# Two heads' scores interleaved from both halves of TensorE's rows, buffers rearranged, and a pinned order in the grouped-query stage

## The chip, the cores and the metric

One NeuronCore of one Trainium2 chip runs the whole program. The metric is device microseconds of one execution. The kernel before took 1280.51 us as the median of three runs, from 1273.82 to 1281.13.

The engines are named as in the profile: PE is TensorE's matmuls, PEld its weight loads, DVE is VectorE, ACT is ScalarE, POOL is GpSimd and SP is SyncE, which issues the DMAs. A line number such as L175 is a line of the kernel before.

## What is computed

The reference is a two-layer encoder on x of 512 tokens by 1024 channels (float32), with four kinds of attention, each with 8 query heads of 64 channels:

- Layer 0, A: attention over the 128 best keys of each query, chosen by an indexer whose scores are sums over 4 small heads; B: chunked attention with a learned bias by distance. Both outputs are concatenated, projected and added to x.
- Layer 1, C: causal attention whose logits get F[t] - F[s], a cumulated log forget gate; D: a sliding window with sinks, where 8 query heads share 2 key heads (grouped queries, 4 heads to a key head). Concatenated, projected, added.
- After each mixer a gated MLP with a causal depthwise convolution, and RMSNorm ahead of every block and at the end.

In every head the logits are q.k over 64 channels, then a softmax over the keys, then P.v. Blocks of 128 queries are used; block i needs keys 0 to 128(i+1), so its logits are 128 x 128(i+1).

## The kernel before

**Precision and matmuls.** Every float32 operand is split into a high and a low part of a reduced format. A product takes three matmuls (`mm3`, L174 to L177): high x high, high x low, low x high, all into one accumulator bank of 128 x 512 (PSUM has 8 banks; `banks` gives 3 to the tag "acc", 3 to "s" and 2 to "tp").

**Weights.** `Stream` loads weights in the order of `PLAN`, 128 x 1024 at a time, through SP's queue into two "raw" buffers; ACT makes the high part (L135) and DVE, for two kinds POOL, the low part (L137). `W.ahead(2)` keeps up to two loads ahead of use.

**Fill work.** Projections are written as Python generators. `Fill.step(n)` runs n steps; one step is three 512-column matmuls for the projections (q and k of the next heads, the queries of D, v of A, output projections). Fill is set between the parts of the attention heads, so that TensorE has work while ACT, DVE and POOL do a softmax. The numbers of steps are written by hand: `FILL_B`, `FILL_A`, `FILL_C`, `FILL_D`.

**A head (B, A and C).** `Head.score` makes four score tiles, of 128, 256, 384 and 512 columns, in three "s" banks, 12 matmuls in all. A pair of heads shares a tile `qk`: head 0 lies in partitions 0 to 63, head 1 in 64 to 127 (`r0`), so that a score matmul uses 64 of the 128 rows of the array. `Head.soft` adds the bias and takes the minimum (DVE), exponentiates (ACT), takes the reciprocal (DVE) and scales (POOL). `Head.turn` transposes P on TensorE into a "tp" bank and `hilo` (L181 to L183) splits it: ACT writes the high part, DVE the low part. `Head.av` multiplies by v into an "acc" bank and `Head.store` sums the two halves of that bank with ACT and DVE.

`weave(prev, cur, fill, n)` (L462) sets the order for one head: transposes of the head before, scores and softmax of this head, then fill in three parts with the remaining transposes and the P.v of the head before in between.

The top-128 choice of A (`topk`, L608 and L609, on DVE) is written behind the B heads. In the trace it runs from 46 to 146 us, beside B.

**C's bias.** `bias_c` selects one row of F with a matmul of 40 rows (`sel`, L874) into a "tp" bank; ACT and POOL make the four bias tiles of one head from it.

**D.** `Unit(i, g)` treats one block of 128 queries and one key head: 12 score matmuls of 64 rows, in two "s" banks, softmax of four heads, transposes, P.v into an "acc" bank. The key head g picks the row half (`r`). Eight units follow one another, with fill of the output projection of C between them.

**What sets the order.** A framework schedules the program: it simulates it, and on each engine issues what is ready, by the order of the source where several are. So an engine's instruction order is that of the simulated schedule and not of the source, while each engine runs its own queue strictly in order. The matmuls of the indexer (L579 to L584), which do the same for its own heads as the change does for the attention heads, show this: they are written in pairs, one matmul for each row half, into two banks:

```
for pas, (x, y) in enumerate(((0, 0), (0, 1), (1, 0))):
    for e in range(2):
        r = slice(64 * e, 64 * e + 64)
        nc.tensor.matmul(ss_[e], iq[r, x, hp, i * 128:w], ik[r, y, 0, 0:w], ...
```

and in the trace some of them stand in this order and some with all three of one e first.

Of the kernel before, what the change touches and what calls it, by code (L numbers as in the profile page):

```python
# [61 lines left out]
def ffn_plan(layer):  # L62
# [4 lines left out]
    for g in range(NFF):  # L67
# [18 lines left out]
def trunk(ctx, tc, a, out):  # L86
# [9 lines left out]
    banks = {"acc": 3, "s": 3, "tp": 2}  # L96
# [4 lines left out]
    h = hp.tile([128, KD, SEQ], F32, name="h")  # L101

    def load_x(c):
        nc.sync.dma_start(h[:, c, :], a["x"][:, c, :])
# [69 lines left out]
    def mm3(o, lh, ll, rh, rl, start, stop):  # L174
        nc.tensor.matmul(o, lh, rh, start=start, stop=False)  # L175
        nc.tensor.matmul(o, lh, rl, start=False, stop=False)  # L176
        nc.tensor.matmul(o, ll, rh, start=False, stop=stop)  # L177
# [20 lines left out]
    for i in range(9):  # L198
        nc.tensor.matmul(wt[:, :128], ones, ones, start=i == 0, stop=i == 8)
# [3 lines left out]
    def squares(c):  # L203
        if c == 0:
            hold_ss["t"] = sp.tile([128, SEQ], F32, name="scr2", tag="scr2", bufs=2)
            nc.scalar.activation(hold_ss["t"], h[:, 0, :], AF.Square, scale=1.0 / 32.0)
            return
        ss = hold_ss["t"]
        sq = sp.tile([128, SEQ], F32, name="os", tag="os", bufs=1)
        nc.scalar.activation(sq, h[:, c, :], AF.Square, scale=1.0 / 32.0)  # L210
# [3 lines left out]
    def squares_ahead():  # L214
        a2 = None
        for p in range(KD // 2):
            sq = sp.tile([128, 2, SEQ], F32, name="scr", tag="scr")
            nc.scalar.activation(sq, h[:, 2 * p:2 * p + 2, :], AF.Square, scale=1.0 / 32.0)
# [8 lines left out]
    def absorb(c, n, sq=True):  # L227
        g = gT[:, n, c:c + 1]
        nc.scalar.activation(xT[0][:, c, :], h[:, c, :], AF.Copy, scale=g)  # L229
        nc.vector.scalar_tensor_tensor(xT[1][:, c, :], h[:, c, :], g, xT[0][:, c, :].bitcast(F32),  # L230
                                       op0=OP.mult, op1=OP.subtract)
        if sq:
            squares(c)

    def token_roots():
        pt = bank("tp", (128, NT))
        for t in range(NT):
            nc.tensor.matmul(pt[:, t:t + 1], hold_ss["t"][:, t * 128:(t + 1) * 128], ones[:, 0:1],  # L238
# [3 lines left out]
    def roots(t0=0, t1=NT, copy=True):  # L242
# [5 lines left out]
        nc.tensor.matmul(pr[:, :n], ones, dg[:, :n], start=True, stop=True)  # L248
# [95 lines left out]
    def add_resid(c, o, cols=slice(0, SEQ)):  # L344
        nc.vector.tensor_tensor(h[:, c, cols], o[:, cols], h[:, c, cols], OP.add)  # L345
# [46 lines left out]
    class Head:  # L392
        def __init__(self, mp, job, ybufs):
            self.mp, self.job, self.ybufs = mp, job, ybufs
            self.where = {}

        def begin(self):
            self.nm = smp.tile([128, NT], F32, name="nm", tag="s4")
            self.sm = smp.tile([128, NT], F32, name="sm", tag="s4")
            P = self.mp.tile([128, 1280], F32, name="P", tag="P", bufs=2)  # L400
            self.L = [P[:, 64 * i * (i + 1):64 * (i + 1) * (i + 2)] for i in range(NT)]

        def score(self):
            qk, r0 = self.job["qk"], self.job["r0"]
            both = bank("s")
            self.s = [both[:, 0:128], both[:, 128:384], bank("s")[:, :384], bank("s")]
            for i, s in enumerate(self.s):
                w = 128 * (i + 1)
                q0, q1 = [qk[r0:r0 + 64, b, 0, i * 128:w] for b in range(2)]
                k0, k1 = [qk[r0:r0 + 64, b, 1, 0:w] for b in range(2)]  # L410
                mm3(s, q0, q1, k0, k1, True, True)

        def soft(self, i):
            s = self.s[i]
            L, nm, sm = self.L[i], self.nm[:, i:i + 1], self.sm[:, i:i + 1]
            nc.vector.tensor_tensor_reduce(out=L, in0=s, in1=self.job["bias"][i], scale=1.0, scalar=3e38,
                                           op0=OP.add, op1=OP.min, accum_out=nm)
            nc.scalar.activation(L, L, AF.Exp, scale=-1.0, bias=nm, accum_out=sm)
            nc.vector.reciprocal(sm, sm)
            nc.gpsimd.tensor_scalar(L, L, sm, 1.0, op0=OP.mult, op1=OP.mult)  # L420

        def turn(self, pk):
# [3 lines left out]
            for j in pk:  # L426
                at[j] = off
                for i in range(j, NT):
                    nc.tensor.transpose(pt[:, off:off + 128], self.L[i][:, j * 128:(j + 1) * 128], ident)
                    off += 128  # L430
            th = self.mp.tile([128, 512], F32R, name="PTh", tag="PTh", bufs=3)
            tl = self.mp.tile([128, 512], F32R, name="PTl", tag="PTl", bufs=3)
            hilo(th[:, :off], tl[:, :off], pt[:, :off])
            for j in pk:
                self.where[j] = (th, tl, at[j])

        def av(self, js, first, last):
            if first:
                self.o = bank("acc")
            for j in js:  # L440
                th, tl, off = self.where[j]
                n = 512 - 128 * j
                v = self.job["V"][:, j].rearrange("p a d -> p (a d)")
                st, sp_ = first and j == js[0], last and j == js[-1]
                nc.tensor.matmul(self.o[:, j * 128:512], v, th[:, off:off + n], start=st, stop=False)
                nc.tensor.matmul(self.o[:, j * 128:512], v, tl[:, off:off + n], start=False, stop=sp_)

        def store(self):
            job, o = self.job, self.o
            e = job["e"]  # L450
# [696 lines left out]
```

## Time and profile before

| | |
|---|---|
| runs | 1273.82, 1280.51, 1281.13 us |
| profiled execution | 1283.04 us, of which the profile's span is 1281.3 us |
| busy in the span | PE 98%, PEld 80%, DVE 64%, ACT 46%, POOL 15% |
| matmuls | 5904 |
| mean granted TensorE clock | 0.986 of full speed |

The span has these stretches: to 72 us loading, the indexer and v of B; 72 to 150 us the B heads; 150 to 290 us the A heads; then layer 0's MLP; 690 to 718 us layer 1's first projections; 718 to 820 us the C heads; 820 to 884 us D; then output projection and MLP. A busy time is the union of the instructions' times; a matmul's time includes its way through the array, so that the distance between the starts of neighbours, not their duration, is what one costs in a row of many.

### The profile page before, as it was taken

The page shows a single profiled execution, that of the slowest core. Times are in us where ns is not written, and L with a number is a line of the kernel's source. Part 1 is how long each engine was busy: PE and PEld are TensorE (multiplying, and loading weights), DVE is VectorE, ACT ScalarE, POOL GpSimd, SP SyncE. Part 2 cuts the span into 40 slices and gives each one's busy share as a digit, 9 for nine tenths or more (in the row PEclk, how much of TensorE's full clock was granted, in tenths as well). Part 3 has the DMA queues.
Part 4 walks back from the last instruction along what each step waited for, and adds up shares of the span by engine and source line. Part 5 has one row for each costly group of instructions (what it writes and reads, how often), then busy time and mean ns, then how long its engine had stood idle before and what let it go on. Part 6 is the DMA issues. An engine that isn't in the chain of part 4 may idle for free. (4 is left out here: it accounts for less than half of the span.)

```text
span 1281.3 us, 15910 instructions
## 1 busy us (share of the span) xinstructions
PE 1256.6 (98%) x5904; PEld 1028.6 (80%) x5904; DVE 824.4 (64%) x1524; ACT 589.1 (46%) x1008; POOL 196.2 (15%) x275
## 2 busy tenths in 40 slices
PE   8999999999999999999999999999999999999997
PEld 7778878787888888888888777778788888888886
DVE  7989866667777777743325556677777777772222
ACT  6445455455544444432224556566544444442221
POOL 3446412212000000000011334212200000000000
PEclk9989999998999999999999999899999999999999
DMA  6222022312233333332222311211223333332221
GB/s 209 83 83 89 28 66 66 99 50 85 85 97 98 99 99 99 99 97 93 92 69 78 116 50 34 66 34 48 89 98 99 99 99 99 98 97 90 96 80 66
DMA packets 34221, 109.61 MB, mean 86 GB/s; under 512 B 4064, under 2 KB 6496, under 8 KB 34144
## 3 DMA queue, kind: packets, MB, share of 16 engines
q1 hardware_dynamic: 34144, 108.60, 26.6%
q8 instruction: 46, 0.75, 0.2%
q14 instruction: 31, 0.25, 0.1%
HBM read 106.49 MB, written 2.10 MB: 85 GB/s over the span
## 5 line engine op out<-in xcount | busy, mean ns | idle before, releaser
L137 DVE TENSOR_TENSOR wlo<-raw,whi 128x1024 fp32r<-128x1024 f32 (+2 forms) x188 | 233.3, 1242 | 152.6 <-ACT whi L135 149.6
L135 ACT ACTIVATE whi<-raw 128x1024 fp32r<-128x1024 f32 (+2 forms) x196 | 204.6, 1044 | 216.3 <-PE acc L176 139.3
L175 PE MATMUL acc<-xT,whi 128*128 128x512 f32 x480 | 189.9, 396 | 0.4 <-ACT xT L229 0.4
L176 PE MATMUL acc<-xT,whi 128*128 128x512 f32 x480 | 188.4, 392 | 1.8 <-DVE xT L230 1.8
L177 PE MATMUL acc<-xT,wlo 128*128 128x512 f32 x480 | 187.9, 391 | 0.0
L212 POOL TENSOR_TENSOR scr<-scr,os 128x512 f32<-128x512 f32 x24 | 34.3, 1430 | 724.5 <-ACT os L210 724.5
L177 PE MATMUL acc<-act,wlo 128*128 128x512 f32 (+1 forms) x374 | 140.9, 377 | 0.0
L175 PE MATMUL acc<-act,whi 128*128 128x512 f32 (+1 forms) x374 | 140.9, 377 | 0.0
L176 PE MATMUL acc<-act,whi 128*128 128x512 f32 (+1 forms) x374 | 140.9, 377 | 0.0
L175 PE MATMUL s<-xT,whi 128*128 128x512 f32 x352 | 139.0, 395 | 0.0
L176 PE MATMUL s<-xT,whi 128*128 128x512 f32 x352 | 137.9, 392 | 0.0
L177 PE MATMUL s<-xT,wlo 128*128 128x512 f32 x352 | 137.8, 392 | 0.0
L175 PEld LDWEIGHTS acc<-xT,whi 128*128 128x128 f32 x480 | 90.8, 189 | 23.1 <-issue 4.1
L176 PEld LDWEIGHTS acc<-xT,whi 128*128 128x128 f32 x480 | 90.9, 189 | 21.0 <-DVE xT L230 2.5
L177 PEld LDWEIGHTS acc<-xT,wlo 128*128 128x128 f32 x480 | 90.7, 189 | 19.2
L175 PE MATMUL acc<-whi,xT 128*128 128x512 f32 (+2 forms) x208 | 83.6, 404 | 1.1 <-ACT whi L135 0.8
L710 DVE TENSOR_TENSOR ov<-s,R 128x512 f32<-128x512 f32 x44 | 30.4, 692 | 80.0 <-PE s L177 80.0
L177 PE MATMUL acc<-whi,xT 128*128 128x512 f32 (+2 forms) x208 | 80.7, 389 | 1.0 <-DVE xT L230 1.0
L182 ACT ACTIVATE act<-scr 128x512 fp32r<-128x512 f32 x44 | 27.8, 631 | 115.7 <-DVE scr L734 115.7
L176 PE MATMUL acc<-wlo,xT 128*128 128x512 f32 (+2 forms) x208 | 80.5, 388 | 0.4 <-DVE wlo L137 0.4
L177 PEld LDWEIGHTS acc<-act,wlo 128*128 128x128 f32 x374 | 70.4, 188 | 13.0
L175 PEld LDWEIGHTS acc<-act,whi 128*128 128x128 f32 x374 | 70.4, 188 | 12.9
(230 smaller groups left out, 2351.2 us busy)
## 6 DMA issues: line engine op xcount, KB each, us to landing
raw<-in_w SPq DMA_DIRECT2D x188, 512.0 KB, 3.5
h<-in_x SPq DMA_DIRECT2D x8, 256.0 KB, 3.9
T<-in_relb SPq DMA_DIRECT2D x8, 256.0 KB, 2.7
raw<-in_w_i SPq DMA_DIRECT2D x4, 324.0 KB, 3.6
raw<-in_w_d SPq DMA_DIRECT2D x4, 264.0 KB, 2.7
out_y<-h SPq DMA_DIRECT2D x4, 256.0 KB, 2.2
out_y<-h SPq DMA_DIRECT2D x2, 384.0 KB, 2.4
ropeC<-in_ropeC SPq DMA_DIRECT2D x2, 256.0 KB, 4.6
```

The lines of the kernel that those rows point to most:

```text
L135: nc.scalar.activation(hi[:, :w], raw[:, :w], AF.Copy)
L137: eng.tensor_tensor(lo[:, :w], raw[:, :w], hi[:, :w].bitcast(F32), OP.subtract)
L175: nc.tensor.matmul(o, lh, rh, start=start, stop=False)
L176: nc.tensor.matmul(o, lh, rl, start=False, stop=False)
L177: nc.tensor.matmul(o, ll, rh, start=False, stop=stop)
L182: nc.scalar.activation(dh, src, AF.Copy)
L212: eng.tensor_tensor(ss, ss, sq, OP.add)
L710: nc.vector.tensor_tensor(v, o, R, OP.mult)
```

## The change

- **Heads in pairs.** `Head` becomes `Pair`. `Pair.score` issues the 24 score matmuls of two heads. Head 0 goes through its tiles in the order 256, 384, 128, 512 columns, head 1 in 384, 128, 512, 256; the two lists are merged by the columns that each has behind it. Each is put behind the matmul traced before it by `tc.keep_in_program_order` (an order of issue on the engine, no wait). The scores fill four "s" banks and two "tp" banks (the 256-column tiles); the two heads never share a bank.
- **Units in pairs.** `Unit(i)` takes both key heads; its 24 score matmuls alternate between the row halves, each pair of the same size, in four "s" banks.
- **Buffers.** "acc" has 2 banks and "s" 4. P.v goes to a "tp" bank. The softmax of a pair is in pieces (`begin`, `rest`, `soft(e, rows)`), the 256-column row first, so that P has a small buffer with four copies and a large one with two; the split transposes have 2 buffers of 512 columns and 1 of 256 where there were 3 of 512. VB (v of B) takes the place of the residual `h`, and x is loaded once more (8 DMAs on SP) after the first A pair.
- **`weave`** has seven parts of fill with shares `PARTS` (D: `PARTS_D`), and the step counts are new. `topk` no longer stands behind a full run of the fill; v of A, the second q and k group of A and B's output projection are in one fill list.
- **C's bias.** `forget_row` uses 128 rows and an "s" bank, and three matmuls a pair (512, 256 and 512 columns) where there were two of 512.
- **D pinned.** From the weave of C's last pair with D's first unit on, `pe.pinned` puts every TensorE instruction behind the one traced before it, until D's units are done.

The core of the diff:

```diff
-FILL_B = (9, 11, 9, 8, 8, 19, 8, 7)
-FILL_A = (22, 17, 10, 10, 11, 6, 5, 3)
-FILL_C = (6, 15, 11, 8, 8, 9, 7, 15)
-FILL_D = ((1, 1, 1, 1), (1, 1, 1, 1), (1, 1, 2, 0), (1, 1, 1, 1),
-          (1, 1, 1, 1), (1, 1, 1, 1), (0, 2, 2, 2), (1, 2, 2, 0))
+FILL_B = (8, 20, 21, 22, 22)
+FILL_A = (23, 30, 16, 14, 11)
+FILL_C = (6, 18, 16, 15, 12)
+FILL_D = (10, 9, 9, 9, 8)
+PARTS = (0, 20, 40, 50, 60, 72, 90, 100)
+PARTS_D = (0, 35, 45, 55, 55, 90, 100, 100)
...
-    banks = {"acc": 3, "s": 3, "tp": 2}
+    banks = {"acc": 2, "s": 4, "tp": 2}
...
+    class Ordered:
+        pinned = False
+        def _do(self, fn, *x, **kw):
+            ins = fn(*x, **kw)
+            if self.pinned:
+                tc.keep_in_program_order(ins)
+            return ins
...
+        def score(self):
+            qk = self.job["qk"]
+            one = [bank("tp") for _ in range(2)]
+            two = [bank("s") for _ in range(2)]
+            three = [bank("s") for _ in range(2)]
+            self.s = [[two[e][:, 0:128], one[e][:, :256], two[e][:, 128:512], three[e]]
+                      for e in range(2)]
+            todo = []
+            for e, order in ((0, (1, 2, 0, 3)), (1, (2, 0, 3, 1))):
+                at = 0
+                for i in order:
+                    for n, (b, c) in enumerate(((0, 0), (0, 1), (1, 0))):
+                        todo.append((at, e, i, n, b, c))
+                        at += i + 1
+            last = None
+            for _, e, i, n, b, c in sorted(todo):
+                w = 128 * (i + 1)
+                r = slice(64 * e, 64 * e + 64)
+                ins = pe.matmul(self.s[e][i], qk[r, b, 0, i * 128:w], qk[r, c, 1, 0:w],
+                                       start=n == 0, stop=n == 2)
+                if last is not None:
+                    tc.keep_in_program_order(ins)
+                last = ins
...
+        if prev is not None:
+            prev.turn(0, 0)
         if cur is not None:
             cur.score()
+            for e in range(2):
+                cur.begin(e)
+                cur.soft(e, (1,))
+        if prev is not None:
+            prev.turn(0, 1)
+        if cur is not None and cur.early:
+            for e in range(2):
+                cur.rest(e)
+                cur.soft(e, (2, 0, 3))
         fill.step(parts[0])
+        if prev is not None:
+            prev.turn(0, 2)
+        if cur is not None and not cur.early:
+            cur.rest(0)
+            cur.soft(0, (2, 0, 3))
+        if prev is not None:
+            prev.av(0, 0)
         fill.step(parts[1])
         if prev is not None:
+            prev.av(0, 1)
+            prev.store(0)
+        if mid is not None:
+            mid(0)
         fill.step(parts[2])
+        if prev is not None:
+            prev.turn(1, 0)
+        fill.step(parts[3])
+        if prev is not None:
+            prev.turn(1, 1)
+        fill.step(parts[4])
...
-        VB = mp.tile([128, NT, 8, 2, HD], F32R, name="VS", tag="VS", bufs=1)
+        VB = hp.tile([128, NT, 8, 2, HD], F32R, name="VB", tag="h")
...
+            if p == 0:
+                H["h"] = hp.tile([128, KD, SEQ], F32, name="h", tag="h")
+                for c in range(KD):
+                    load_x(c)
...
+        def forget_row(hh, w):
+            sel = mp.tile([128, 128], F32R, name="sel", tag="PSh", bufs=1)
...
+            pb = bank("s")
+            pe.matmul(pb[:, :w], sel, FTh[:, :w], start=True, stop=True)
...
+                for u in range(2):
+                    for e in range(2):
+                        for n, (b, c) in enumerate(((0, 0), (0, 1), (1, 0))):
+                            for g in range(2):
+                                r = slice(64 * g, 64 * g + 64)
+                                ins = pe.matmul(self.s[u][g][:, e, :nk], qd[u][r, b, e, qs],
+                                                       kdT[r, c, k0:k0 + nk], start=n == 0, stop=n == 2)
...
+        for i in range(NT + 1):
...
+            pe.pinned = True
+            cur = Unit(i) if i < NT else None
+            weave(pend, cur, fill, FILL_D[i], share=PARTS_D if i else PARTS)
+            pend = cur
+        pe.pinned = False
```

## Rows read from the trace of the kernel before

**Rows 1.** Windows, one stretch of the MLP: length, busy time (count) by engine, clock, DMA.
```profile
360.00:400.00 40.00, 40.00 (x178) 33.14 (x177) 29.06 (x37) 18.31 (x23) 0.00 (x0) 1.00 0.29 93
```

**Rows 2.** Windows, layer 0's heads, and within them the first 10 us and 92 to 142.
```profile
72.00:292.00 220.00, 214.67 (x1075) 174.54 (x1076) 167.73 (x444) 112.69 (x255) 72.24 (x100) 0.98 0.21 65
72.00:82.00 10.00, 7.07 (x19) 5.52 (x20) 8.47 (x29) 4.42 (x10) 3.30 (x6) 0.66 0.26 81
92.00:142.00 50.00, 50.00 (x261) 41.40 (x259) 48.81 (x139) 26.63 (x63) 32.82 (x40) 1.00 0.25 80
```

**Rows 3.** Windows, C and D, and within them 830 to 840.
```profile
718.00:884.00 166.00, 162.02 (x786) 123.40 (x785) 111.37 (x325) 106.94 (x275) 55.01 (x102) 0.96 0.15 48
830.00:840.00 10.00, 10.00 (x41) 7.90 (x40) 5.96 (x23) 4.77 (x16) 1.10 (x3) 0.68 0.12 48
```

**Rows 4.** Waits of PE: waiting <- releaser, us in total, times, longest.
```profile
PE s L175 <- ACT qk L491: 2.2, 2, 1.9
PE s L176 <- POOL qk L492: 2.1, 2, 1.1
...
PE acc L445 <- ACT PTh L182: 1.6, 1, 1.6
```

**Rows 5.** Timeline of PE, scores of one B head: start, length, what, count.
```profile
87.58 0.32 PE L175 MATMUL s<-qk 64*128 64x128 f32 x1
...
89.68 0.50 PE L175 MATMUL acc<-xT,whi 128*128 128x512 f32 x1
...
91.86 0.38 PE L429 MATMUL tp<-ident,P 128*128 128x128 f32 x2
```

**Rows 6.** Timeline of PE, the indexer's scores, window 55.50 to 55.60.
```profile
55.54 0.50 PE L582 MATMUL s<-qk 64*128 64x512 f32 x2
```

**Rows 7.** Timeline of PE, the same, window 56.28 to 56.30.
```profile
56.11 0.40 PE L582 MATMUL s<-qk 64*128 64x512 f32 x2
```

**Rows 8.** Timeline of PE, the same, window 56.51 to 56.54.
```profile
56.34 0.39 PE L582 MATMUL s<-qk 64*128 64x512 f32 x1
```

**Rows 9.** Timeline of PE, scores of one unit of D.
```profile
844.67 0.38 PE L175 MATMUL s<-kdT,qk 64*128 64x256 f32 x1
...
846.30 0.50 PE L175 MATMUL acc<-yT,whi 128*128 128x512 f32 x1
```

**Rows 10.** Timeline of PE, last score matmul of a parted C head, and next fill.
```profile
733.31 0.50 PE L177 MATMUL s<-qk 64*128 64x512 f32 x1
733.73 0.50 PE L175 MATMUL acc<-xT,whi 128*128 128x512 f32 x1
```

**Rows 11.** Timeline of PE, what parts the first parted head (in A).
```profile
176.03 0.63 PE L429 MATMUL tp<-ident,P 128*128 128x128 f32 x4 [0.29 <-DVE qk L183]
```

**Rows 12.** Timeline of PE, what parts the last parted head (in C).
```profile
806.66 0.66 PE L429 MATMUL tp<-ident,P 128*128 128x128 f32 x4
```

**Rows 13.** Timeline of PE, one selection of F for a C head.
```profile
758.98 0.50 PE L874 MATMUL tp<-FTh,sel 40*128 40x512 f32 x1
759.41 0.66 PE L429 MATMUL tp<-ident,P 128*128 128x128 f32 x4
```

**Rows 14.** Tile tp: duration in ns min/median/max, first and last start.
```profile
L182 ACT ACTIVATE PTh<-tp x86: 359/592/617, 87.2 to 882.3; 128x512 fp32r<-128x512 f32 x62, 128x256 fp32r<-128x256 f32 x24
L183 DVE TENSOR_TENSOR PTl<-tp,PTh x86: 395/680/692, 88.4 to 883.1; 128x512 fp32r<-128x512 f32 x62, 128x256 fp32r<-128x256 f32 x24
```

**Rows 15.** Groups of DVE, window 820 to 884: count, busy us, mean ns.
```profile
L956 DVE CUSTOM_DVE_ANT_0 P<-s,dmask,nsink 128x256 f32<-128x256 f32 x24 | 10.9, 477 | 1.6 <-PE s L177 1.6
...
L1003 DVE TENSOR_TENSOR Y<-acc,Y 64x512 f32<-64x512 f32 x7 | 4.8, 688 | 2.5 <-ACT Y L1002 2.4
```

**Rows 16.** Line 609, the choice of the top keys: durations, first and last start.
```profile
L609 DVE MATCH_REPLACE8 wk<-m,wk x48: 401/543/679, 46.5 to 145.7; 128x256 f32<-128x256 f32 x16, 128x384 f32<-128x384 f32 x16, 128x512 f32<-128x512 f32 x16
```

**Rows 17.** DMA issues: count, KB each, median us to landing.
```profile
raw<-in_w SPq DMA_DIRECT2D x188, 512.0 KB, 3.5
h<-in_x SPq DMA_DIRECT2D x8, 256.0 KB, 3.9
```

More of the change, by code (lines that the diff above doesn't have):

```diff
@@ L198, in trunk @@
     for i in range(9):
-        nc.tensor.matmul(wt[:, :128], ones, ones, start=i == 0, stop=i == 8)
+        pe.matmul(wt[:, :128], ones, ones, start=i == 0, stop=i == 8)
     hold_ss = {}
@@ L247, in roots @@
         pr = bank("tp", (128, NT, 128))
-        nc.tensor.matmul(pr[:, :n], ones, dg[:, :n], start=True, stop=True)
+        pe.matmul(pr[:, :n], ones, dg[:, :n], start=True, stop=True)
         if copy:
@@ L390, in load_rope @@
         nc.sync.dma_start(ropeS, a["ropeS"])
-    class Head:
+    class Pair:
         def __init__(self, mp, job, ybufs):
             self.mp, self.job, self.ybufs = mp, job, ybufs
[L395 to L401, printed above, removed]
-        def score(self):
[L404 to L407, printed above, removed]
-                w = 128 * (i + 1)
[L409 to L422, printed above, removed]
@@ L423, in turn @@
+        def turn(self, e, n):
+            pk = ([0], [1, 3], [2])[n]
             pt = bank("tp")
@@ L433, in turn @@
+            th = self.mp.tile([128, w], F32R, name=tag + "h", tag=tag + "h", bufs=bufs)
+            tl = self.mp.tile([128, w], F32R, name=tag + "l", tag=tag + "l", bufs=bufs)
             hilo(th[:, :off], tl[:, :off], pt[:, :off])
             for j in pk:
[L435 to L446, printed above, removed]
@@ L448, in store, with av @@
-        def store(self):
-            job, o = self.job, self.o
-            e = job["e"]
+                self.where[e][j] = (th, tl, at[j])
+        def av(self, e, n):
+            if n == 0:
+                self.o[e] = bank("tp")
+            o = self.o[e]
+            for j in ([0, 1, 3], [2])[n]:
+                th, tl, off = self.where[e][j]
+                w = 512 - 128 * j
+                v = self.job["V"](e)[:, j].rearrange("p a d -> p (a d)")
+                pe.matmul(o[:, j * 128:512], v, th[:, off:off + w], start=j == 0, stop=False)
+                pe.matmul(o[:, j * 128:512], v, tl[:, off:off + w], start=False, stop=j == 2)
@@ new lines, in trunk, with next_b, f @@
+        nb = {hh: bias_b(hh)() for hh in range(2)}
+        fill.step(FILL_B[0])
+        def next_b(p):
+            def f(e):
+                if p < 3:
+                    nb[2 * p + 2 + e] = bias_b(2 * p + 2 + e)()
+            return f
+        for p in range(4):
+            job = dict(qk=pairs[p]["qk"], pair=pairs[p], V=lambda e, p=p: VB[:, :, 2 * p + e],
+                       bias=[nb.pop(2 * p + e) for e in range(2)])
+            cur = Pair(mp, job, 2)
+            weave(pend, cur, fill, FILL_B[p + 1], next_b(p))
+            pend = cur
@@ new lines, in trunk @@
+        for i in (1, 2, 3):
+            topk(i)
+        later.drain()
+        for p in range(4):
+            if p == 2:
+                later.drain()
+            job = dict(qk=qkA[p], pair=pairs[4 + p], V=lambda e, p=p: VA["t"][:, :, 2 * p + e],
+                       bias=[[cmask, work[1], work[2], work[3]]] * 2)
+            cur = Pair(mp, job, 2)
+            weave(pend, cur, fill, FILL_A[p])
+            if p == 0:
+                H["h"] = hp.tile([128, KD, SEQ], F32, name="h", tag="h")
+                for c in range(KD):
+                    load_x(c)
+            pend = cur
@@ L697, in trunk @@
         fill.add(out_half("oA", lambda k: pairs[4 + k]["y"], after=lambda c: absorb(c, 1), lead=(0, 1, 2)))
-        weave(pend, None, fill, 11)
+        weave(pend, None, fill, FILL_A[4])
         fill.run()
@@ L912, in trunk, with next_c, f @@
         pend = None
-        nb = {0: bias_c(0)()}
-        fill.step(2)
-        for hh in range(8):
-            p = hh // 2
-            job = dict(qk=pairs[p]["qk"], r0=64 * (hh % 2), e=hh % 2, pair=pairs[p],
-                       V=VC[:, :, hh], bias=nb.pop(hh))
-            head = Head(mp, job, 1)
-            weave(pend, head, fill, FILL_C[hh])
-            if hh < 7:
-                nb[hh + 1] = bias_c(hh + 1)()
-            pend = head
-        fill.run()
+        bias_first(0)
+        fill.step(FILL_C[0])
+        def next_c(p):
+            def f(e):
+                if e == 0:
+                    bias_second(p)
+                elif p < 3:
+                    bias_first(p + 1)
+            return f
+        for p in range(4):
+            job = dict(qk=pairs[p]["qk"], pair=pairs[p], V=lambda e, p=p: VC[:, :, 2 * p + e], bias=cbias[p])
+            cur = Pair(mp, job, 1)
+            weave(pend, cur, fill, FILL_C[p + 1], next_c(p))
+            pend = cur
         Yds = {}
@@ L976, in turn @@
+            def turn(self, g, n):
                 if n >= len(self.blocks):
```

343 lines of the change are left out of this document (166 added, 177 removed).

## The prediction

> **What bounds the kernel now.** I read first the windows of the trace. In a stretch of the MLP TensorE starts 178 matmuls of 512 columns in 40 us at full clock: 0.225 us each, without a pause [rows 1]. The change doesn't touch those stretches. In layer 0's heads TensorE is busy 214.67 of 220 us and the clock is 0.98 of full [rows 2]; in C and D it is busy 162.02 of 166 us and the clock 0.96 [rows 3]. So TensorE bounds the attention stages too, and time can come from three places: fewer matmul slots, less lost where TensorE changes between kinds of matmul, and the idle and slow-clock time. The last is small: 5.3 + 4.0 us idle, and (220 x 0.02) + (166 x 0.04) = 11.0 us by the clock, 20.3 us together. The list of waits says what the idle time waited for: mostly the first heads' q and k, and one P.v on ACT [rows 4].
>
> **What a head's scores cost.** The 12 score matmuls of a B head begin at 87.58 and the next fill at 89.68, 2.10 us; the nine fill matmuls behind them take 2.18 us up to 91.86, where nine at 0.225 would take 2.02 [rows 5]. The 0.16 us more is the way back from 64-row to 128-row matmuls. A head costs 2.26 us, and the 24 heads 54.2 us.
>
> **What two halves of the array do at once.** The indexer's 512-column matmuls show it. Where its source order (one half, then the other) survived, two start together and both are through in 0.50 us [rows 6], or in 0.40 us further on [rows 7]; the next starts 0.23 us after such a pair [rows 8]. That is the slot of a single 512-column matmul (0.225 us [rows 1]). So two equal matmuls on different halves cost one slot.
>
> **Part by part.**
> *Pairs of heads.* 24 blocks become 12. If one head runs wholly beside the other, a pair costs what one head costs: 12 x 2.26 = 27.1, gain 27.1 us. But the two lists here have different sizes side by side, which the trace before doesn't show for attention heads. Bounds: all side by side, gain 27.1; all in sequence, a pair costs 2 x 2.10 + 0.16 less the 0.2 us of one change of kind (0.42 against 0.22, [rows 10]), 4.16 us, gain 54.2 - 49.9 = 4.3. A loss is excluded, because the number of blocks is halved either way. The nearest rows are the equal pairs, so I take nearly all of it, 25.6 us: short matmuls of head 1 that start behind a long one of head 0 may have to wait for its end. When I step through the 24 in merged order at 0.23 us for 512 columns and let none end before an earlier one, a pair takes 0.25 us more; half of that times 12 is the 1.5 us taken off. By TensorE: Matmul & The Clock Gate, Part 3, in the Trainium skill, matmuls are strictly first in, first out in start and in end; by that the gain would be 24.1 instead of 27.1. The rows show equal ends only.
> *Pairs of units.* Here equal sizes alternate, as in rows 6 and 7. A unit's scores take 844.67 to 846.30, 1.63 us [rows 9], plus 0.16: 1.79. Eight become four: gain 7.2 us.
> *Parted blocks.* Often the scheduler has put transposes between scores. The last score matmul of such a head, alone behind transposes, takes 0.42 us until the next fill starts instead of 0.22 [rows 10], and the exit of the first piece adds 0.16: 0.36 us a piece. From the first [rows 11] to the last [rows 12] I count 13 extra pieces in 11 of the 24 heads, and 9 more in D. Pinning ends those of D. The heads' scores are chained among themselves only, so other matmuls may still stand between them; I keep half. Gain (9 + 6) x 0.36 = 5.4, between 3.2 and 7.9.
> *F's rows.* A selection takes 0.43 us to the next start [rows 13] and an exit of 0.16: 8 x 0.59 = 4.7. With 128 rows it is no change of kind: 8 x 0.225 + 4 x 0.12 (half the columns) = 2.3. Gain 2.4.
> Sum of these: 40.6 us.
> *First waits.* 72 to 82 us lost 2.9 us idle and 3.4 us by the clock (0.66) [rows 2]: scores waited for ACT and POOL to split q and k [rows 4]. Now 8 steps of fill stand before the first B scores instead of 4, and 6 instead of 2 before C's: 4 x 3 x 0.225 = 2.7 us more cover. I count 5 us of this as gained.
> *The "tp" ring.* Transposes, the 256-column scores and P.v all take turns in two banks. A turn is 0.59 us on ACT and 0.68 on DVE after the transposes [rows 14], about 1.3 us. In A, B and C fill can be scheduled into it. In D it can't: behind `store(0)` come `turn(1, 0)` and `turn(1, 1)` with no fill between them, and the second needs the bank that the store frees. The store is 0.6 us on ACT and 0.69 on DVE [rows 15], behind the DVE's eight bias operations of 0.48 us for the next unit; its cover is four transposes. I take 1.9 us of wait for each of four weaves, 7.5 us, between 0 and 15. What waits behind it is every matmul, since the order is pinned.
> *Clock after such waits.* After a wait of 1.6 us on ACT [rows 4] the clock stood at 0.68 from 830 to 840 [rows 3], 3.2 us lost; I take 5 us for D.
> The remaining waits of A, B and C I put at 7 us, so that waits and clock come to 19.5 us after and 20.3 before (the 5 us of the first waits are in this): gain 0.8.
> *At no cost.* Reloading x is 8 DMAs of 256 KB on SP, each 3.9 us to landing [rows 17]; behind them are weight loads for v of A and its second q and k group, which are two loads ahead, 2 x 24 x 0.225 = 10.8 us; eight in a row at what the 512 KB loads take (3.5 us each) would be 14 us at most, so without cover 3 us. SP also waits there for the last P.v of B. Two "acc" banks serve groups of 24 matmuls, 5.4 us, against 1.3 us of emptying.
>
> **Sum.** 40.6 + 0.8 = 41.4 us. The profiled execution took 1283.0 us (span 1281.3); 1283.0 - 41.4 = 1241.6. The median is 2.5 us below it: **1239 us**.
>
> **Rivals.**
> *DVE sets B's pace.* From 92 to 142 us DVE is busy 48.81 of 50 us [rows 2], because the choice of top keys runs until 145.7 [rows 16]. B's saving (4 x 2.26 and the first wait, about 14 us) would then only bring A's first scores ahead of their bias. For it: there is no slack on DVE. Against it: 23 fill steps (15.5 us) stand between A's first scores and the transposes that need them. Time: 1239 + 14 = 1253. TensorEngine Tiling (Array Packing), PSUM Bottleneck, in the Trainium skill warns of this: tiling speeds up TensorE and not the emptying of PSUM, which may become the bound. In this trace DVE's 98% bears that out for B alone; in layer 0's heads as a whole it is 76%.
> *Unequal sizes don't overlap.* Gain 4.3 instead of 25.6: 1239 + 21 = 1260. Nothing in the trace excludes it.
> *The pairs come apart.* Other matmuls could be issued between the chained scores, as in rows 10 to 12. With six pieces in each of 12 pairs, 5 x 0.36 x 12 = 22 us go, and part of the overlap, some 10 us: 1270. Then the change doesn't do what it says.
> *D at the slow clock, slower than before.* D's pinned weaves hold about 55 us of TensorE work (64 us from 820 to 884, plus 10 fill steps and a head moved in, less the gains above). If each weave's wait is like the one before 830, so that the clock stays at 1.2 GHz until the fill after D, the 55 us double: 1239 + 55 = 1294. It decides from the point where four weaves in a row wait over 1.6 us; half of D at that clock would be 1266. Against it: over C and D together the clock before was 0.96 of full, with waits in it [rows 3].
>
> **Chances.** Forecast (1218 to 1250) 0.58; DVE in B 0.17; sequence 0.11; apart 0.06; D slow 0.08, of which a quarter stops short of slower. About 1% (13 us) is what a measurement of this kernel can tell from no change. Faster by over 1% (below 1267.7): 0.58 + 0.17 + 0.11 = 0.86. Within 1%: 0.06 + 0.02 = 0.08. Slower: 0.06. The range goes from all new waits and the end-order loss absent (1239 - 19.5 - 1.5 = 1218) to the sequence rival, 1260, and the 2 us by which the parted blocks may fall short: 1218 to 1262.
>
> **What the profile after would show.** Right: a pair's 24 scores within 2.0 to 2.3 us from first start to next fill; starts of both halves within some nanoseconds in D; about 16 blocks of 64-row attention scores; F's selection at 0.23 us; the mean clock no lower than before. Wrong: 24 scores in 3.8 us or more; top keys done after A's first transposes should start; PE waits on ACT or DVE in each of D's weaves, with a clock below 0.8 there; a wait for weights behind the loads of x. What would break the forecast most is a scheduled order in A, B and C that fits the simulated times and not the real ones.

## The result and the profile after

The changed kernel took 1262.03 us as the median of four runs (1261.7 to 1262.71), the kernel before 1277.75 us on the same chip: a ratio of 0.9879 (0.9843 to 0.9914), faster by 1.2%. Beside other experiments it ran again at 0.9842 (0.9828 to 0.9857). The forecast was 1239 us with a range to 1262. The direction was right; 20 of the 41 us that it counted on are missing. One execution of `seq` below took 2031.81 us at a granted clock of 0.556; no ratio contains it. Line numbers from here on are those of the changed kernel, where every matmul is L106 and the tiles tell them apart.

The windows answer to [rows 2]: columns are the stretch, its length, the busy time (count) of PE, PEld, DVE, ACT and POOL, the granted clock, and the DMA's share and GB/s.

```profile
72.00:82.00 10.00, 7.98 (x43) 6.58 (x43) 9.72 (x29) 4.91 (x9) 3.80 (x4) 0.83 0.27 85
92.00:142.00 50.00, 43.20 (x236) 35.03 (x234) 49.21 (x136) 23.15 (x54) 25.13 (x31) 0.97 0.21 67
72.00:292.00 220.00, 205.63 (x1111) 167.25 (x1111) 180.30 (x452) 122.70 (x265) 79.55 (x104) 0.98 0.25 80
781.60:890.50 108.90, 91.16 (x516) 75.01 (x516) 80.88 (x197) 64.06 (x158) 25.55 (x33) 0.94 0.18 56
```

From 92 to 142 us DVE is as full as before (49.21 of 50 us), and TensorE, which had no pause there [rows 2], now stands still for 6.8 us. In D and the output projection (last line) TensorE is idle for 17.7 of 108.9 us, at a clock of 0.94. The waits of PE answer to [rows 4] (who waits <- for whom, us in total, times, longest):

```profile
PE tp L106 <- DVE Y L1111: 12.1, 5, 6.3
PE tp L106 <- DVE PTl L201: 7.7, 7, 3.9
PE s L106 <- ACT VS L200: 3.1, 1, 3.1
PE acc L106 <- DVE h L363: 3.0, 3, 1.7
...
PE tp L106 <- ACT qk L564: 1.1, 1, 1.1
...
PE tp L106 <- POOL qk L565: 0.9, 1, 0.9
```

The waits for the split of q and k, 2.2 and 2.1 us in [rows 4], are down to 1.1 and 0.9. What stands ahead now is DVE: the store of a unit of D, and the low part of transposed P.

The scores themselves do what was forecast. The timeline of PE (start, length, what, count) shows a pair of heads, answering to [rows 5]:

```profile
146.35 0.38 PE L106 MATMUL tp<-qk 64*128 64x256 f32 x1
146.35 0.44 PE L106 MATMUL s<-qk 64*128 64x384 f32 x1
...
148.47 0.66 PE L106 MATMUL tp<-ident,P 128*128 128x128 f32 x4
```

Two matmuls of unequal size start together, and all 24 are through in 2.12 us, where one head alone took 2.10. Seven of the twelve pairs of heads take 2.1 to 2.2 us; in the other five a wait of 0.4 to 3.9 us falls between the scores, though no other matmul does. A pair of units, answering to [rows 9], takes 1.62 us for 24 matmuls where one unit took 1.63:

```profile
797.30 1.69 PE L106 MATMUL s<-kdT,qk 64*128 64x256 f32 x24
798.92 0.50 PE L106 MATMUL acc<-whi,xT 128*128 128x512 f32 x1
```

**Where the time went.** I split the span by stage into idle time (no matmul on record), time lost by the clock (half of the busy time at 1.2 GHz, where a slot of 512 columns took 0.43 us, for example at 828.21, and not 0.225), and the rest, which I call work. Layer 0's heads are here the stretch from 72 us to the end of the first output projection, 238.7 us long before and 226.5 after.

| stage | idle + clock before, us | after, us |
|---|---|---|
| layer 0's heads | 6.8 + 5.1 = 11.9 | 14.4 + 3.4 = 17.8 |
| C | 1.9 + 1.7 = 3.6 | 3.2 + 0 = 3.2 |
| D and output projection | 2.8 + 5.1 = 7.9 | 17.7 + 4.8 = 22.5 |
| all else | 13.2 + 3.4 = 16.6 | 13.0 + 0.6 = 13.6 |
| span | 40.0 | 57.1 |

The span fell by 21.4 us (1281.3 to 1259.9), so work fell by 21.4 + 17.1 = 38.5 us; the forecast had 40.6. This is a remainder; counted directly, the slots of the scores (from each start to the next matmul's, less idle time and the clock's part) fell from 67.7 to 33.6 us. Waits and clock were to be 0.8 us less and are 17.1 us more.

**D's largest wait.** The timeline of PE, with the idle time ahead of an instruction and its releaser in brackets:

```profile
801.09 0.39 PE L106 MATMUL tp<-PTh,VD 128*128 128x512 f32 x1
801.32 0.40 PE L106 MATMUL tp<-PTl,VD 128*128 128x512 f32 x1
801.55 0.60 PE L106 MATMUL tp<-ident,scr 128*128 128x128 f32 x4
...
802.46 0.39 PE L106 MATMUL acc<-yT,wlo 128*128 128x512 f32 x1
809.20 1.09 PE L106 MATMUL tp<-ident,P 128*128 128x128 f32 x4 [6.35 <-DVE Y L1111]
```

P.v of a unit and the transposes of D's next queries hold both tp banks; the next transposes need one back. DVE's timeline shows why it comes so late:

```profile
802.48 0.47 DVE L1063 CUSTOM_DVE_ANT_0 PP<-s,dmask,nsink 128x256 f32<-128x256 f32 x1
...
804.32 0.67 DVE L358 TENSOR_TENSOR scr<-acc,ropeC 128x512 f32<-128x512 f32 x1
...
805.72 1.20 DVE L155 TENSOR_TENSOR wlo<-raw,whi 128x1024 fp32r<-128x1024 f32 x1
...
808.39 0.66 DVE L1111 TENSOR_TENSOR Y<-tp,Y 64x512 f32<-64x512 f32 x1
```

P.v is done by 801.7, but ahead of the store in DVE's queue stand the next unit's softmax, the rotation of D's queries and a low part of weights. TensorE's order is pinned, so fill that is ready stays behind the wait.

**B's largest wait** has the same form with other work in DVE's queue:

```profile
98.17 0.38 PE L106 MATMUL tp<-qk 64*128 64x256 f32 x1 [3.94 <-DVE PTl L201]
```
```profile
94.54 0.54 DVE L682 MATCH_REPLACE8 wk<-m,wk 128x384 f32<-128x384 f32 x1
95.11 0.56 DVE L681 MAX8 m<-wk 128x8 f32<-128x384 f32 x1
...
97.44 0.67 DVE L201 TENSOR_TENSOR PTl<-tp,PTh 128x512 fp32r<-128x512 f32 x1
98.03 0.41 DVE L456 CUSTOM_DVE_ANT_0 P<-tp,T 128x256 f32<-128x256 f32 x1
```

Head 1's 256-column score tile needs the bank of the first transposes. ACT had made their high part by 95.1; DVE's low part stood behind top-key operations until 97.44.

### The profile page after: what moved, and what is told of

Its sections match the earlier page's. It is cut to its first block, busy times and chain, and to the rows that moved or that the text cites. A ratio compares the mean times of both kernels' runs of the same rounds, so it can differ in the third digit from the quotient of the medians.

```text
span 1259.9 us, 15944 instructions
## 1 busy us (share of the span) xinstructions
PE 1211.5 (96%) x5908; PEld 999.1 (79%) x5908; DVE 829.6 (66%) x1528; ACT 593.1 (47%) x1008; POOL 199.4 (16%) x275
## 4 chain that ended last, share of the span: by engine, by line
PE 73%; DVE 14%; ACT 5%; issue 3%; DMA 2%; POOL 1%; SPq 0%; POOLq 0%; DVEq 0%; ACTq 0%
PE acc L106 48%; PE s L106 21%; PE tp L106 5%; DVE wlo L155 2%; DVE wk L682 2%; DVE m L681 2%; ACT whi L153 1%; DMA raw<-in_w 1%; DVE P L456 1%; DVE PTl L201 1%; ACT P L458 1%; DVE xT L248 1%; DMA h<-in_x 1%; DVE scr L358 1%; DVE wk L664 1%
## 5 line engine op out<-in xcount | busy, mean ns | idle before, releaser
L106 PE MATMUL acc<-xT,whi 128*128 128x512 f32 x960 | 299.3, 393 | 0.8 <-DVE h L363 0.4
L106 PE MATMUL acc<-act,whi 128*128 128x512 f32 (+1 forms) x748 | 219.5, 377 | 0.0
L106 PE MATMUL s<-xT,whi 128*128 128x512 f32 x704 | 217.4, 390 | 0.0
L106 PEld LDWEIGHTS acc<-xT,whi 128*128 128x128 f32 x960 | 179.6, 189 | 38.6 <-issue 1.9
L106 PE MATMUL acc<-xT,wlo 128*128 128x512 f32 x480 | 187.5, 391 | 0.0
L106 PEld LDWEIGHTS acc<-act,whi 128*128 128x128 f32 x748 | 137.7, 188 | 25.8
L106 PEld LDWEIGHTS s<-xT,whi 128*128 128x128 f32 x704 | 132.1, 188 | 28.5 <-issue 0.7
L106 PE MATMUL acc<-whi,xT 128*128 128x512 f32 (+2 forms) x416 | 143.9, 399 | 2.0 <-DVE xT L248 1.0
L106 PE MATMUL acc<-act,wlo 128*128 128x512 f32 (+1 forms) x374 | 140.9, 377 | 0.0
L106 PE MATMUL s<-xT,wlo 128*128 128x512 f32 x352 | 137.5, 391 | 0.0
L106 PEld LDWEIGHTS acc<-xT,wlo 128*128 128x128 f32 x480 | 90.6, 189 | 18.9
L106 PEld LDWEIGHTS acc<-whi,xT 128*128 128x128 f32 x416 | 78.4, 189 | 17.5 <-DVE xT L248 1.5
L106 PE MATMUL acc<-wlo,xT 128*128 128x512 f32 (+2 forms) x208 | 80.8, 389 | 1.3 <-DVE wlo L155 1.3
L106 PEld LDWEIGHTS acc<-act,wlo 128*128 128x128 f32 x374 | 70.3, 188 | 12.9
L106 PEld LDWEIGHTS s<-xT,wlo 128*128 128x128 f32 x352 | 66.0, 188 | 13.8 <-issue 0.2
L779 ACT ACTIVATE scr<-ov,cw 128x512 f32<-128x512 f32 x88 | 71.3, 810 | 2.3 <-DVE ov L778 1.5
L458 ACT ACTIVATE P<-P,nm 128x256 f32<-128x256 f32 (+3 forms) x96 | 53.4, 558 | 37.1 <-DVE nm L456 36.5
```

The costliest lines, as they stand in the source:

```text
L106: ins = fn(*x, **kw)
L779: nc.scalar.activation(dst, v, AF.Identity, scale=cw[:, c, 2:3], bias=cw[:, c, 3:4])
```

## The experiments

Theory: the overlap works as forecast, and two groups of waits on DVE eat nearly half of what the change saves: in B behind the top-key choice, in D because the pinned order leaves no fill to run meanwhile. Rivals: the overlap is worth less than forecast; the tp ring alone is at fault; the pinned order is innocent, since the simulated schedule doesn't see these waits. Each edit is made to the changed kernel; ratios are to the kernel before on the same chip.

**1. No overlap.** In `Pair.score`:
```
-            for _, e, i, n, b, c in sorted(todo):
+            for _, e, i, n, b, c in todo:
```


> The changed kernel, but all 12 score matmuls of head 0 of a pair are issued before those of head 1; banks, fill and everything else as changed. If the two row halves really run side by side, each of the 12 pairs now takes about 4.0 us instead of 2.1, and if TensorE bounds the attention stages this costs 12 x 1.9 = 23 us: ratio to the kernel before about 1.006. Rival: the pair's time is hidden behind waits that DVE sets, so that taking the overlap away costs under 8 us and the idle time falls by what the scores grow.

> All twelve scores of head 0 before those of head 1, as in the run seq, for a trace that can be read. Theory 'overlap works, its gain is partly lost in waits': the 24 scores of a pair take 3.8 to 4.2 us to the next work instead of 2.1, so that slots of scores grow by 12 x 1.7 = 20 us, while TensorE's idle time falls from 41 us to below 30, because a wait on a tp bank then is covered by the longer scores; the ratio comes out at 0.988, as in seq. Rival 'the order of the two lists makes no difference to the overlap': scores of a pair take about 2.1 to 2.5 us here too, and idle time stays at about 41 us.

> The changed kernel itself, to stand beside the others of this call on one chip. 0.988 of the kernel before (0.984 to 0.991), some 1262 us, idle time of TensorE about 41 us.

`seq` gave 0.9886 (0.9865 to 0.9907), far from my 1.006, so it was run again beside the changed kernel: 1268.09 us, 0.9882 (0.9867 to 0.9897), against 1262.68 us, 0.9842. The overlap is worth 5.4 us. In sequence the 24 matmuls take 3.28 us:

```profile
94.89 0.62 PE L106 MATMUL tp<-qk 64*128 64x256 f32 x3
95.35 2.54 PE L106 MATMUL s<-qk 64*128 64x384 f32 x18
97.73 0.52 PE L106 MATMUL tp<-qk 64*128 64x256 f32 x3
98.17 0.66 PE L106 MATMUL tp<-ident,P 128*128 128x128 f32 x4
```

Against the changed kernel beside it, the slots of the scores grow by 12.2 us over the span (33.6 to 45.8), idle time falls from 47.6 to 42.0 and the clock's loss from 11.3 to 9.3 us. So the overlap does save 12 us of TensorE's time, and 7.6 us of that is given back in waits and clock: the wait on `PTl` is 2.7 us here, 7.1 there. Expected were 20 us; in sequence a pair costs less than the 3.8 that I allowed.

**2. A shorter top-key choice.** In `topk`:
```
-            for r in range(TOPK // 8):
+            for r in range(TOPK // 32):
```
This leaves out 12 of the 16 rounds, so that 32 keys are chosen and not 128.

> The changed kernel with 4 of the 16 rounds of the top-128 choice, so that 32 keys are chosen and 12 rounds of three DVE operations for each of three blocks are left out. Theory: in the B heads TensorE waits at the end of a pair's scores for a bank whose emptying stands in DVE's queue behind that choice; without it the idle time from 72 us to the A heads falls from 8.8 to under 4 us and the time by 5 to 8 us. Rival: the wait comes from the ring of two banks itself; then the waits stay and the time falls by less than 2 us.

> Both edits at once: 4 of the 16 rounds of the choice of top keys (leaves out 12 rounds) and all scores of head 0 ahead of head 1. Theory 'the overlap pays in full where no wait follows it': without the top-key queue on DVE there is little idle time left in the first layer's heads that longer scores could fill, so the step from topk4 to this run is 9 to 12 us (0.9763 of before to 0.984 to 0.986), more than the 5.4 us from changed_again to seq_again; idle time falls by less than 2 us from topk4's 33.5. Rival 'the overlap is worth some 5 us whatever follows': 0.9805.

`topk4` gave 0.9763 (0.9744 to 0.9781), 1251.58 us, a larger gain than the 5 to 8 us expected. Layer 0's heads went from 226.5 to 214.1 us, their idle time from 14.4 to 6.7, the clock's loss from 3.4 to 0. The window to set against the second line of the first fence:

```profile
92.00:142.00 50.00, 49.94 (x284) 41.98 (x284) 30.63 (x89) 28.46 (x68) 27.36 (x35) 1.00 0.18 58
```

DVE drops to 30.63 us and TensorE does 284 matmuls where it did 236. The wait on `PTl` falls from 7.7 to 1.0 us, though the ring of two tp banks is as it was. So DVE set B's pace, and that costs 12 us. With the scores in sequence as well (`seq_topk4`) the ratio is 0.9854 (0.9825 to 0.9883): without DVE's queue the same loss of overlap costs 0.9854 - 0.9763 = 0.9%, give or take 0.3%, or 12 us, and not 5.4. The overlap pays in full where no wait follows it.

**3. D's store and DVE's queue.** In `Unit.av`, and in `Unit`:
```
-                    self.o[g] = bank("tp", (128, 4, 128))
+                    self.o[g] = bank("acc", (128, 4, 128))
```
```
-            early = True
+            early = False
```


> The changed kernel, but in the grouped-query stage P.v is written to a bank of the tag acc, as before the change, instead of tp. Theory: TensorE's waits there (16 us idle) come from transposes that need the tp bank which the store of the first key head frees; with its own bank the waits on that store vanish from the list (12.1 us before) and the time falls by 6 to 12 us. Rival 1: only two acc banks are left for fill and P.v, so the wait moves to the fill matmuls and nothing is gained. Rival 2: P itself is late; then the transposes wait on POOL or ACT instead.

> The changed kernel, but in the grouped-query stage the softmax of a unit's two key heads is written in two places, the first after the transposes of the unit before, the second behind that unit's first store, instead of both at once behind the scores. Theory: the store of the first key head waits on ACT and DVE behind the whole softmax of the next unit; with half of it in front the wait on that store falls from 12.1 us by half or more and the time by 4 to 10 us. Rival: the queues' order is set by readiness and not by the place in the source, so nothing moves (under 2 us).

> Both edits to the grouped-query stage at once: P.v into the acc banks, and the second key head's softmax written behind the transposes. Theory (two waits of their own: the tp ring, and DVE's queue of the next unit's softmax): together they save more than the better one alone, ratio 0.974 to 0.979 (after alone 0.988, acc_out 0.979, late_soft 0.982), idle in D and the output projection below 11 us. Rival (both free the same wait): no better than acc_out, 0.979, idle about 12 us.

`acc_out` (first edit) gave 0.9792 (0.9772 to 0.9812), `late_soft` (second) 0.9815 (0.9794 to 0.9835), both together (`acc_late`) 0.9751 (0.9735 to 0.9766), 1251.09 us. The second edit alone cuts the wait on the store from 12.1 to 7.3 us, not by the half that was expected. D and the output projection took 103.5, 107.7 and 99.6 us for 108.9. Together they save 9.3 us there, more than 5.4 and 1.2 one by one: bank and queue each hold the wait. In `acc_out` the wait on the tp bank is gone, and a part comes back on the acc banks, behind the same softmax on DVE:

```profile
PE acc L106 <- DVE sm L1074: 3.7, 1, 3.7
PE acc L106 <- DVE es L1071: 3.1, 1, 3.1
```

**4. Other orders.** `scores_first` puts `cur.score()` and its first softmax ahead of `prev.turn(0, 0)` in `weave`; `fill_between` puts fill between `turn(1, 0)` and `turn(1, 1)` of D:
```
-PARTS_D = (0, 35, 45, 55, 55, 90, 100, 100)
+PARTS_D = (0, 35, 45, 55, 75, 90, 100, 100)
```


> In every weave the next pair's scores are issued ahead of the first transposes of the pair before, not behind them; nothing else is changed. Theory (what is late is DVE's part of the first turn, behind its top-key operations and the softmax): the 256-column tiles then find both tp banks free and are not held by the first turn; B's wait of 3.95 us at 98 us goes, and about 3 to 6 us in all: ratio 0.983 to 0.986. Rival (the wait moves to the first turn, which then waits for the bias operation on the 256-column tile on the same DVE): ratio 0.987 to 0.992, the wait for a tp bank stands at the transposes.

> In D two of the fill steps that stood behind the last transposes of the second key head stand between its first and its second transposes, where the prediction saw the wait for the bank that the store frees. Theory (a matter of cover): the three or four waits there shrink by up to 2 x 0.67 us each, 3 to 5 us in all, ratio 0.980 to 0.984; the wait at 826 us falls from 3.8 to about 2.5 us. Rival (DVE is late by more than the cover and the fill is missing later, in front of P.v): less than 1.5 us, 0.983 to 0.986.

`scores_first`: 0.9862 (0.9834 to 0.989), between the two expected ranges and no better than the changed kernel. The rival's mechanism held: the wait moved to DVE's softmax on the 256-column tile (`nm` L456, 11.0 us in all), and layer 0's heads took 232.1 us. `fill_between`: 0.9836 (0.981 to 0.9862), inside both expected ranges. The wait at 826 us is 2.52 us where it was 3.80, the largest stays 6.3, and D with the output projection takes 105.7 us for 108.9, which is the theory's gain; but layer 0's heads, which the edit doesn't touch, were 3 us longer in this profile, and the medians can't decide it.

**5. Without the pinned order.** The line `pe.pinned = True` is taken out; the chains inside the scores stay.

> The grouped-query stage without the pinned order (the scores of a pair of units stay chained); nothing else. Theory 'pinning makes the waits': the scheduler puts fill into the waits, idle in D and the output projection falls from 17.7 to below 8 us, while parted score blocks come back (some 5 x 0.36 us): ratio 0.978 to 0.982. Rival 'the simulated schedule does not see these waits': idle stays within 3 us of 17.7 and the ratio is 0.984 to 0.990.

`unpinned_d` gave 0.9725 (0.9701 to 0.9749), 1245.59 us: more than the theory expected, 15 to 17 us from one line. D and the output projection take 95.1 us where `changed_again` took 110.2. The window over them, and the waits of PE in them:

```profile
780.70:875.70 95.00, 90.84 (x520) 72.29 (x520) 80.03 (x199) 64.70 (x159) 25.36 (x34) 1.00 0.21 64
```
```profile
PE acc L106 <- DVE h L363: 1.3, 2, 0.9
PE acc L106 <- DVE scr L358: 0.9, 1, 0.9
```

Idle falls from 17.7 to 4.2 us, and the clock stays at 2.4 GHz. The scheduler parts the score blocks again, with fill and transposes between, which costs 2.4 us (the slots of the scores rise from 33.6 to 36.0 us over the span):

```profile
808.30 0.61 PE L106 MATMUL s<-kdT,qk 64*128 64x256 f32 x5
808.85 0.66 PE L106 MATMUL tp<-ident,P 128*128 128x128 f32 x4
809.43 0.74 PE L106 MATMUL s<-kdT,qk 64*128 64x256 f32 x8
810.20 0.63 PE L106 MATMUL tp<-ident,scr 128*128 128x128 f32 x4
```

The rival that the simulated schedule doesn't see these waits is refuted.

**6. Do the causes add, and can DVE be eased?** `unpin_topk4` is `unpinned_d` with the shorter choice of 2, again with 32 keys. In the others POOL makes the low part of layer 0's head outputs, by the edit below in `Pair.store`: `eased` adds it to `acc_late`, `unpin_ypool` to `unpinned_d`; `unpin_all` is `unpin_ypool` with both edits of 3, and `unpin_ypool_wpool` is `unpin_ypool` with `'qB'` added to the weights whose low part POOL makes.
```
-                hilo(y[:, 0], y[:, 1], Y)
+                nc.scalar.activation(y[:, 0], Y, AF.Copy)
+                eng = nc.gpsimd if self.ybufs == 2 else nc.vector
+                eng.tensor_tensor(y[:, 1], Y, y[:, 0].bitcast(F32), OP.subtract)
```


> acc_late (P.v of D in the acc banks, the second key head's softmax behind the transposes) and the low part of layer 0's head outputs made by POOL in place of DVE. Theory (in B, DVE's queue is what TensorE waits for; 4 x 1.29 us leave it there): idle in the first layer's heads falls from 15.0 (acc_late) to 10 to 12 us, ratio 0.971 to 0.973 against acc_late's 0.975. Rival (only the total of the top-key operations counts, or POOL's 1.37 us operations come late for the output projection): within 1 us of acc_late, 0.974 to 0.976.

> No pinned order in D, and 4 of the 16 rounds of the choice of top keys (leaves out 12 rounds). Theory (two separate causes make up the whole of what the forecast missed: the pinned order of D, some 15 us, and DVE's queue behind the top-key operations in B, some 12 us): the gains add up, ratio 0.960 to 0.964 of before (0.9725 and 0.9763 alone, the changed kernel 0.984 to 0.988), some 1233 us, idle 20 to 23 us. Rival (one cause shows in both, or one stage only waits for the other): no lower than 0.968.

> No pinned order in D, and the low part of layer 0's head outputs on POOL in place of DVE. Theory (gains of separate stages add up): 3 to 5 us less than unpinned_d (0.9725), 0.969 to 0.970. Rival (POOL's later end or the 5 us off DVE's queue matter only together with acc_late's other order): 0.972 to 0.974.

> unpin_ypool with D's P.v in the acc banks and the second key head's softmax behind the transposes. Theory (those two edits only answer waits of the pinned order; without it the scheduler covers them with fill): within 2 us of unpin_ypool. Rival (the tp ring and DVE's softmax queue cost time without pinning too): 3 to 5 us below unpin_ypool, 0.966.

> unpin_ypool with the low part of the q weights of B also on POOL: 4 x 1.22 us off DVE, 4 x 2.40 us onto POOL, most of it before 92 us. Theory (every us off DVE ahead of the last top key is a us off B): 2 to 4 us below unpin_ypool. Rival (POOL's 2.40 us makes the weights late, or the stretch before 92 us is not bound by DVE): 0 to 2 us slower than unpin_ypool.

| run | median, us | ratio | 95% | idle + clock: heads of layer 0; D |
|---|---|---|---|---|
| `eased` | 1247.48 | 0.9741 | 0.9712 to 0.977 | 14.5; 11.0 |
| `unpin_topk4` | 1238.43 | 0.9676 | 0.9656 to 0.9695 | 11.8; 4.2 |
| `unpin_ypool` | 1243.39 | 0.9721 | 0.9703 to 0.9739 | 14.3; 4.2 |
| `unpin_all` | 1243.89 | 0.9725 | 0.9708 to 0.9742 | 15.8; 5.1 |
| `unpin_ypool_wpool` | 1247.39 | 0.9751 | 0.9732 to 0.9771 | 16.8; 4.2 |

`unpin_topk4` is at 1238 us. That this is near the forecast's 1239 is chance: the kernel does less work. It misses the 0.960 to 0.964 of full addition and stands at the rival's 0.968. D's part adds in full (95.1 us, as in `unpinned_d`). In layer 0's heads, 218.9 us against 214.1 in `topk4`, the order of instructions is the same; what differs is one wait of 1.77 us at 114 us (last section), a spell of 3.4 us at 1.2 GHz behind it and another at 279 us, each of which costs 1.7 us. So, stage by stage, the causes add but for this. `unpin_all` is no better than `unpin_ypool`: the edits of 3 only answered waits that the pinned order made. POOL in place of DVE for the head outputs gains 1.3 us by the ratios of `acc_late` and `eased` and 0.5 us by those of `unpinned_d` and `unpin_ypool`, within the intervals. In the profiles layer 0's heads take 223.2 to 224.7 us with it in three runs, and 226.0 to 229.7 in the seven that touch nothing there; so a gain of the expected 3 to 5 us is hinted at, but not shown. More work on POOL made it worse by 4 us. With the full choice of top keys the lowest are `unpin_ypool` and `unpinned_d`, 0.972 of before; both beat the changed kernel.

Not run were the shorter choice of top keys on the kernel before, and the new fill steps and buffers apart from the pairs; what these alone cost or save stays open.

## Why the prediction missed

**Right: the work.** Pairs of heads (2.12 us a pair), pairs of units (1.62 us) and fewer blocks came out as summed: 38.5 us of work saved against 40.6. I had taken off 1.5 us, half of what matmuls that may not end before earlier ones would cost by my stepping; the pair above shows no such loss, 2.12 us against 2.10. That matmuls end strictly in order is a rule of the Trainium skill (TensorE: Matmul & The Clock Gate, Part 3); since the profile models the ends of matmuls, no run here tests the rule itself. A selection of F with 128 rows costs 0.22 us:

```profile
714.05 0.39 PE L106 MATMUL s<-FTh,sel 128*128 128x512 f32 x1
714.27 0.62 PE L106 MATMUL acc<-xT,whi 128*128 128x512 f32 x2
```

Four of the eight with 512 columns cost 0.30 to 0.34, so not all of the 2.4 us was gained.

**Right: what was to cost nothing.** The reloaded x shows no wait of TensorE, and the rival of pairs coming apart didn't occur. That of unequal sizes was wrong, and overpriced: sequence costs 12 us, not 21, because a pair in sequence takes 3.28 us where my sum had 4.0 without the exit.

**Wrong: "The remaining waits of A, B and C I put at 7 us".** Layer 0's heads and C lost 21.0 us by waits and clock. The mechanism stood among the rivals as *DVE sets B's pace*, with 14 us at a chance of 0.17; the runs put it at 12. [Rows 2] had shown it: with TensorE and DVE both full from 92 to 142 us, work taken from TensorE alone can't shorten that stretch. I argued it away with the cover ahead of A's transposes and looked for the delay at A's bias; the last round of the top keys starts at 136.9 us, and the delay shows inside B, as waits for a tp bank. TensorEngine Tiling (Array Packing), PSUM Bottleneck, in the Trainium skill warned that the emptying of PSUM may become the bound. B's windows agree in part: TensorE waits for banks that DVE has yet to empty, but some 27.6 of DVE's 49.2 us are the choice of top keys and no emptying.

**Wrong in size: "The tp ring", in D.** For D 7.5 us of waits and 5 us of clock were taken; measured are 17.7 and 4.8 with the output projection, so the clock's term held and the waits were too small by 10 us. (It held by luck in part: the spell at 1.2 GHz before lasted from 826.1 to 836.4 us and cost 5.1 us, not the 3.2 that the window of [rows 3] catches.) 12.1 us of them are at the store. The place was right (`turn(1, 1)` behind `store(0)`), DVE's eight bias operations were named, and the sign that I gave for being wrong there, waits on DVE in D's weaves at a low clock, came (1.2 GHz from 805.6 to 812.4 us). What was missed is what else DVE had in front of the store: from 803.90, when the last bias operation is through, to 808.39, 4.5 us of rotation, weights, sums and the queries' low part. A loss by pinning had no term of its own: the prediction did say that every matmul waits behind this one, but counted pinning only as the end of parted blocks. The runs price it at 13.5 us idle and 4.8 to 6.2 us of clock against 2.4 us of whole blocks.

**Wrong in form: the rivals as alternatives.** DVE in B and the waits in D lie in different stages, so they can both come. My range took each rival alone. The two terms were short by 14 us (21.0 for 7) and 10 us; 3.0 us came back in the other stages, 3.1 us were lost before the change too, in stretches that my 20.3 us left out, and with the 2.1 us of work this gives the 20 us that are missing.

## What to carry to other kernels

Before you take work from one engine, look in each stage for the second one that is full: there the saving ends at the other engine's time. Pin an engine's order only where every wait in it is covered by what stands ahead of it; whole blocks of scores were worth 2.4 us here, the freedom to run fill in a wait 18 to 20. And add rivals that lie in different stages.

## What the runs showed of the hardware

Two matmuls of unequal size on the two row halves, into two banks, start together, and 24 of them cost what 12 do (2.12 us, and 2.10 for one head); that was bounded but unknown before.

A DVE subtraction from SBUF to SBUF takes 0.69 us, or over four times that. In `topk4` it starts 0.13 us ahead of POOL's low part of weights, in `unpin_topk4` 0.02 us behind (timelines of both engines):

```profile
111.18 0.69 DVE L201 TENSOR_TENSOR yT<-Y,yT 128x512 fp32r<-128x512 f32 x1 [0.67 <-ACT yT L200]
...
111.31 2.81 POOL L155 TENSOR_TENSOR wlo<-raw,whi 128x1024 fp32r<-128x1024 f32 x1
```
```profile
110.91 2.37 POOL L155 TENSOR_TENSOR wlo<-raw,whi 128x1024 fp32r<-128x1024 f32 x1
110.93 2.90 DVE L201 TENSOR_TENSOR yT<-Y,yT 128x512 fp32r<-128x512 f32 x1 [0.68 <-ACT yT L200]
```

The second DVE operation ends 0.55 us after POOL's, as if it began only then. SBUF — State Buffer, "SBUF: two separate sides", in the Trainium skill says that an operation of DVE with two SBUF inputs and one of POOL that reads SBUF exclude each other, the first to start having its way; the two traces agree. Here 0.15 us of timing decided over 2.2 us on DVE, and with them the wait of 1.77 us on TensorE and 1.7 us by the clock behind it, out of the 4.8 us by which layer 0's heads differed at the same instruction order. D's largest wait seems to hold one more of these: a sum of 128 x 2 on DVE takes 0.14 us, and 1.22 us where POOL is at work on `scr`; both end within 0.02 us of each other, ahead of the store (changed kernel):

```profile
805.24 0.14 DVE L1073 TENSOR_TENSOR sm<-sm,es 128x2 f32<-128x2 f32 x1
...
805.87 2.17 POOL L360 TENSOR_TENSOR scr<-scr 128x512 f32<-128x512 f32 x1 [0.80 <-DVE sm L1074]
...
806.84 1.22 DVE L1073 TENSOR_TENSOR sm<-sm,es 128x2 f32<-128x2 f32 x1
```
